# A hybrid decoder layer: key norms by selector products, packed inversion blocks, decay sums loaded a step ahead, c spread by TensorE and a closing block of 512

## The chip, the cores and the metric

One Trainium2 chip, one core. The metric is the device time of one execution in microseconds (us). Engines: PE is TensorE (matrix products; PEld are its weight loads), DVE is VectorE, ACT is ScalarE, POOL is GpSimd and SP the queue from which most DMA transfers are issued; POOL issues the others.

## The reference, cut to what matters

One decoder layer for 256 tokens of width 2048, all in fp32. Two modulations come from a condition vector c; the token mixer runs attention with 8 heads and a gated delta rule with 16 value heads beside each other; then comes a SwiGLU of inner width 5632.

```python
mod = silu(c) @ w_ada + b_ada                  # 6 x 2048: sh1, sc1, g1, sh2, sc2, g2
h = x * (1.0 + sc1) + sh1
proj = h @ w_in                                # attention q, k, v; delta q, k, v; z, b, a; two gates
y_a = moba_attention(qa, ka, va, rel_bias)     # 256 tokens: one causal block per head
qb, kb, vb = split(silu(causal_conv4(gdn_qkv)))
qb, kb = l2norm(qb) * 128 ** -0.5, l2norm(kb)
beta = sigmoid(gdn_b);  g = -exp(a_log) * softplus(gdn_a + dt_bias)
o = gated_delta_rule(qb, kb, vb, g, beta)      # decays exp(cumsum g), a triangular solve, a running state
y_b = o * rsqrt(mean(o * o) + eps) * gdn_norm_w * silu(z)
merged = sigmoid(gate_a) * (y_a @ w_proj_moba) + sigmoid(gate_b) * (y_b @ w_proj_gdn)
x = layer_norm(ALPHA * x + g1 * (merged @ w_out))
h = x * (1.0 + sc2) + sh2
x = layer_norm(ALPHA * x + g2 * ((silu(h @ w_gate) * (h @ w_up)) @ w_ffn_out))
```

## The kernel before, in words

Every large product keeps fp32 accuracy by splitting both operands into two parts of a reduced fp32 type: `split_w` lets ACT write the high part `hi` of a weight tile of 512 KB and DVE the rest `lo`, and three products (hi x hi, hi x low, lo x high) replace one. A program of steps (`step`, `do`, `run(3)`) holds one weight tile per step: SP loads it into one of six `raw` buffers, ACT and DVE split it up to three steps ahead, and PE multiplies; a step of 24 narrow products is the clock of all else. `raw_a` tiles of w_ada share the `raw` buffers; a DVE sum along them (`ada_sum`) gives one column of the modulation.

The first five groups of steps (`startup`) go through parts of w_in with as many rows of h as are ready: the sums need c, broadcast to all partitions and put through Silu (`load_c`), and `ada_opening` loads its tiles with `between` placing the first part of x and the small weights `wba` among them.

The rest of the token mixer is written as generators in lanes ("moba" for attention, "main" for gates, the delta rule's chain, its norm and transposes, "pre" for convolution, norms and the transposing of v, "ada" for sums). After each step `tick` advances them by a budget: a yielded number is a cost, `rest(n)` lets a lane pause for n steps, so that a transfer may land, and `until(flag)` waits for another lane. A planner then fixes each engine's order; engines take their instructions in that order.

For batch b of 8 value heads: `gdn_qk` sums the squares of q and k on PE (`ss`), sends the sums to DRAM (`rnd`), reads them back as 16 columns, takes the inverse roots, writes them back, and loads them broadcast to all partitions as four tiles `rb`, by which DVE multiplies `kq`. `gdn_chain` then loads, per pair of heads, the decay sums (`gr`), forms the decayed products `ma0` and `ma1`, and inverts a unit triangular matrix per head and chunk: all blocks of 128x128 go to DRAM (`mbd`), their diagonal blocks of 32x32 are gathered as `Mb`, inverted on DVE column by column, scattered to `ubd` and read back as `UU`; PE merges the blocks (`ps_mt`, `z`, `ps_a`) and applies them. Many small tiles share one tag, c2, with four buffers: `gr`, `e`, `rb`, the attention's `bias`, `z`, `tm` and others. In PSUM the tags gd and tp have two buffers each for all lanes.

The last projection (`w_fo`, 5632 rows) runs in column blocks of 512, 512, 512, 256 and 256 (`ln_blocks`); with each block DVE forms the residual, its statistics and a scaling, and after the last `finish` gives the means and inverse deviations. The closing products and eight DVE operations write the output.

## Time and profile before

| | us |
|---|---|
| median of 3 runs | 1732.25 (1728.62 to 1736.27) |
| the profiled execution | 1728.49 |
| its span in the trace | 1726.4 |
| PE, DVE, ACT busy | 1649.9, 1233.1, 831.2 |

The profiled execution has its own time, 2.1 us above the span that the trace covers. A share of busy time is an average over stages. A gap in a time line is put down to the instruction that ended it last. Matrix products overlap in the records, so a standing PE is seen in the idle time before an instruction, and a slow one in the granted clock.

### The profile page before, as it was taken

Reading aid. Unit: us, or ns where it says so; the run is one execution under the profiler, and the core shown is the slowest. Engines: PE = TensorE matmul, PEld = TensorE weight load, DVE = VectorE, ACT = ScalarE, POOL = GpSimd, SP = SyncE. Lnnn points to the kernel's source line nnn. Section 1 sums busy time; section 2 is a strip of 40 time slices with the busy share of each in tenths; the row PEclk is TensorE's granted clock in tenths of the full one; section 3 lists DMA queues with packets and bytes.
Section 4 is the critical chain, followed back from the end, with each engine's and each line's share of the span. In section 5 each row is a group of like instructions: output and inputs, shape, how many; then the busy total and the mean of one; then the engine's idle time right before and its main releaser. Section 6 shows DMA issues by size and latency. Waiting matters only on the chain.

```text
span 1726.4 us, 28691 instructions
## 1 busy us (share of the span) xinstructions
PE 1649.9 (96%) x11317; PEld 1497.8 (87%) x11317; DVE 1233.1 (71%) x1767; ACT 831.2 (48%) x1182; POOL 47.9 (3%) x78
## 2 busy tenths in 40 slices
PE   3999999989998999999999999999999999999997
PEld 3899999779987889889988998888888888888896
DVE  6899999669775568657989787666666666555454
ACT  3544455569453494346433454444444444433341
POOL 0000000111010000000000000000000000000000
PEclk9999999999998999999999999999999999999998
DMA  9999996667676667866999567777777777655651
GB/s 376 349 353 347 368 335 211 200 206 222 196 230 194 191 192 241 277 192 196 313 347 361 170 205 262 234 229 231 228 226 231 231 234 231 227 193 191 195 183 73
DMA packets 115414, 417.52 MB, mean 242 GB/s; under 512 B 13836, under 2 KB 14956, under 8 KB 109772
## 3 DMA queue, kind: packets, MB, share of 16 engines
q1 hardware_dynamic: 110464, 401.17, 68.5%
q0 software_dynamic: 4816, 14.52, 3.3%
q8 instruction: 89, 1.46, 0.3%
q14 instruction: 45, 0.37, 0.1%
HBM read 409.75 MB, written 5.89 MB: 241 GB/s over the span
## 4 chain that ended last, share of the span: by engine, by line
PE 62%; DVE 3%; DMA 3%; issue 1%; ACT 1%; DVEq 0%; POOL 0%; ACTq 0%; POOLq 0%
PE mm L307 17%; PE mm L311 8%; PE mm L348 8%; PE mm L350 7%; PE mm L349 7%; PE mm L302 4%; PE mm L301 4%; PE mm L300 4%; DMA raw_a<-in_w_ada 1%; DVE lo L216 1%; PE ps L721 1%; DMA raw<-in_w_out 1%; ACT hi L215 0%; DMA rb<-rnd 0%; DVE raw_a L235 0%
## 5 line engine op out<-in xcount | busy, mean ns | idle before, releaser
L215 ACT CAST hi<-raw 128x1024 fp32r<-128x1024 f32 (+2 forms) x576 | 582.0, 1015 | 687.6 <-PE mm L350 219.6
L216 DVE TENSOR_TENSOR lo<-raw,hi 128x1024 fp32r<-128x1024 f32 (+2 forms) x576 | 673.1, 1177 | 291.8 <-ACT hi L215 289.7
L300 PE MATMUL mm<-s,hi 128*128 128x256 f32 x1232 | 349.9, 285 | 28.4 <-ACT s L223 23.7
L302 PE MATMUL mm<-s,lo 128*128 128x256 f32 x1232 | 346.9, 282 | 4.8 <-DVE lo L216 4.7
L301 PE MATMUL mm<-s,hi 128*128 128x256 f32 x1232 | 346.8, 282 | 0.0
L307 PE MATMUL mm<-s,hi 128*128 128x512 f32 x1280 | 319.5, 392 | 0.0
L307 PEld LDWEIGHTS mm<-s,hi 128*128 128x128 f32 x1280 | 228.5, 188 | 39.4
L300 PEld LDWEIGHTS mm<-s,hi 128*128 128x128 f32 x1232 | 234.9, 191 | 30.7 <-ACT s L223 23.7
L302 PEld LDWEIGHTS mm<-s,lo 128*128 128x128 f32 x1232 | 235.0, 191 | 6.8 <-DVE lo L216 6.6
L301 PEld LDWEIGHTS mm<-s,hi 128*128 128x128 f32 x1232 | 235.9, 192 | 0.7 <-issue 0.2
L311 PEld LDWEIGHTS mm<-s,lo 128*128 128x128 f32 x1280 | 169.8, 188 | 13.6
L311 PE MATMUL mm<-s,lo 128*128 128x256 f32 x1280 | 171.9, 277 | 0.0
L348 PE MATMUL mm<-hi,ach 128*128 128x512 f32 (+1 forms) x440 | 152.6, 347 | 0.0
L350 PE MATMUL mm<-hi,acl 128*128 128x512 f32 (+1 forms) x440 | 152.5, 347 | 0.0
L349 PE MATMUL mm<-lo,ach 128*128 128x512 f32 (+1 forms) x440 | 152.5, 347 | 0.0
L235 DVE CUSTOM_DVE_ANT_0 raw_a<-raw_a,cb,cols 128x1024 f32<-128x1024 f32 x56 | 71.8, 1283 | 52.0 <-DMA raw_a<-in_w_ada 52.0
L235 DVE CUSTOM_DVE_ANT_0 raw_a<-raw_a,cb,ada_half 128x1024 f32<-128x1024 f32 x56 | 71.8, 1282 | 48.7 <-DMA raw_a<-in_w_ada 48.6
L235 DVE CUSTOM_DVE_ANT_0 r<-r,cb,cols 128x2048 f32<-128x2048 f32 x40 | 93.7, 2346 | 10.6 <-DMA r<-in_w_ada 10.6
L350 PEld LDWEIGHTS mm<-hi,acl 128*128 128x128 f32 x440 | 83.4, 189 | 10.4
L349 PEld LDWEIGHTS mm<-lo,ach 128*128 128x128 f32 x440 | 83.4, 189 | 10.4
L348 PEld LDWEIGHTS mm<-hi,ach 128*128 128x128 f32 x440 | 83.4, 189 | 10.1
L348 PE MATMUL mm<-hi,s 128*128 128x512 f32 x192 | 78.5, 409 | 0.0
(309 smaller groups left out, 2274.3 us busy)
## 6 DMA issues: line engine op xcount, KB each, us to landing
raw<-in_w_ffn_in SPq DMA_DIRECT2D x176, 512.0 KB, 4.4
raw<-in_w_in SPq DMA_DIRECT2D x160, 512.0 KB, 4.5
raw_a<-in_w_ada SPq DMA_DIRECT2D x112, 512.0 KB, 4.4
raw<-in_w_ffn_out SPq DMA_DIRECT2D x88, 512.0 KB, 4.3
r<-in_w_ada SPq DMA_DIRECT2D x40, 1024.0 KB, 8.4
raw<-in_w_in SPq DMA_DIRECT2D x48, 384.0 KB, 6.5
raw<-in_w_proj_gdn SPq DMA_DIRECT2D x32, 512.0 KB, 4.5
raw<-in_w_out SPq DMA_DIRECT2D x32, 512.0 KB, 5.6
```

Of the source, the lines that this page charges most:

```text
L215: s_.copy(hi, raw)
L216: low = v_.tensor_tensor(lo, raw, hi.bitcast(F32), op=OP.subtract)
L235: v_.tensor_tensor_reduce(out=raw, in0=raw, in1=cb[:, n * part:n * part + n], scale=1.0, scalar=cols[:, col:col + 1] if first else h, op0= ...
L300: t_.matmul(o, hi[:, i, c], ah, start=(first and i == 0 and t == 0), stop=False)
L301: t_.matmul(o, hi[:, i, c], al, start=False, stop=False)
L302: t_.matmul(o, lo[:, i, c], ah, start=False, stop=(last and i == kn - 1 and t == 1))
L307: t_.matmul(box[t].rearrange("p (u i) -> p u i", u=2), hi[:, i, t * P:(t + 1) * P], both[k0 + i], start=(first and i == 0), stop=False)
L311: t_.matmul(box[t][:, :S], lo[:, i, t * P:(t + 1) * P], both[k0 + i][:, 0, :], start=False, stop=(last and i == kn - 1))
L348: t_.matmul(box[h], xh, hi[:, i, :], start=start, stop=False)
L349: t_.matmul(box[h], xh, lo[:, i, :], start=False, stop=False)
L350: t_.matmul(box[h], xl, hi[:, i, :], start=False, stop=stop)
L721: t_.matmul(ps[to, n, :], lhs(n), rhs(n), start=True, stop=True)
```

## The change

Six edits. The condition vector is loaded as one row and spread over the partitions by four products with a row of ones; the first part of x follows the four first weight tiles and `wba` comes in the second group. The norms of q and k stay on the chip: the inverse roots are taken on all partitions, split into a high and a low part in `rows`, and selector columns (`sel`) spread them by PE into PSUM, where DVE reads them. `gr` is loaded one pair ahead. Only diagonal blocks, packed by ACT (`mc`), go through DRAM, and three rests are shorter. The squares of the output norm come before z is waited for. The closing projection has four blocks of 512, and the last block's scaling keeps its place in the program, behind `finish`.

```diff
-    c[:, C_SEL + 1] = 1.0
-    c[:, C_QS] = np.where(i < 64, SCALE, 1.0)
+    c[:, C_SEL + 1] = c[:, C_SEL + 17] = 1.0
+    c[:, C_QS] = np.where(i % 16 < 1, SCALE, 1.0)
+    c[:, C_LOW] = np.where(i % 32 < 16, 0.0, -1.0)
...
-    def load_c(i):
-        half = cb[:, 1024 * i:1024 * i + 1024]
-        dma.dma_start(half, a["c"][0, 1024 * i:1024 * i + 1024].partition_broadcast(P))
-        s_.activation(half, half, AF.Silu)
+    def load_c():
+        ones = e2("ones", [1, P])
+        v_.memset(ones, 1.0)
+        dma.dma_start(cb[0:1, :], a["c"])
+        for i in range(4):
+            ps = (pt.tile([P, 512], F32, tag="tp", name="ps_c") if i % 2 else
+                  pg.tile([P, 512], F32, tag="gd", name="ps_c"))
+            t_.matmul(ps, ones, cb[0:1, 512 * i:512 * i + 512], start=True, stop=True)
+            s_.activation(cb[:, 512 * i:512 * i + 512], ps, AF.Silu)
...
-        if n == 2:
+        if n == 2 * GROUPS[0][1]:
             load_x(*GROUPS[0])
-        elif n == 3:
-            load_ba()
...
             do(load_small)
+            do(load_ba)
...
+    def make_sel():
+        for g in range(4):
+            for u in range(2):
+                c = 32 * g + u
+                v_.tensor_tensor(sel[:, g + 4 * u:g + 4 * u + 1], ident[:, c:c + 1], ident[:, c + 16:c + 17], op=OP.add)
...
-        sr = e2("sr", [P, S])
-        s_.copy(sr, ss)
-        for g in range(4):
-            sdma.dma_start(rnd[b][g::4], sr[32 * g:32 * g + 2])
...
+        yield rest(2)
+        nr, nt = c2("nr", [P, 2, S]), c2("nt", [P, S])
+        re, rr = nr[:, 0, :], nr[:, 1, :]
+        v_.tensor_scalar(re, ss, epsc[:, 0:1], None, op0=OP.add)
+        s_.activation(rr, re, AF.Sqrt)
+        yield 0.4
+        yield rest()
+        v_.reciprocal(rr, rr)
+        v_.tensor_tensor(nt, rr, rr, op=OP.mult)
+        v_.tensor_tensor(nt, nt, re, op=OP.mult)
+        v_.tensor_scalar(nt, nt, -0.5, 1.5, op0=OP.mult, op1=OP.add)
+        v_.scalar_tensor_tensor(nt, nt, cst[:, C_QS:C_QS + 1], rr, op0=OP.mult, op1=OP.mult)
+        hi = k1.tile([P, S], F32R, tag="c2", name="nh", bufs=4)
+        s_.copy(hi, nt)
+        v_.scalar_tensor_tensor(rows, hi.bitcast(F32), cst[:, C_LOW:C_LOW + 1], nt, op0=OP.mult, op1=OP.add)
+        yield 2.2
+        for t in range(4):
+            if t % 2 == 0:
+                yield rest()
+                rbs = [pt.tile([P, 2, S], F32, tag="tp", name="rb"), pg.tile([P, 2, S], F32, tag="gd", name="rb")]
+                for x in range(2):
+                    for i in range(2):
+                        n = t + x + 4 * i
+                        t_.matmul(rbs[x][:, i, :], sel[:, n:n + 1].to_broadcast([P, P]), rows, start=True, stop=True)
+                yield 0.1
+                yield rest()
+            v_.tensor_tensor(kq[:, t::4, :], kq[:, t::4, :], rbs[t % 2], op=OP.mult)
             yield 0.6
...
-        for q in range(4):
+        def gc_rows(q):
             gr = c2("gr", [P, 2, S])
             sdma.dma_start(gr, bc_heads(gcd, 8 * b + 2 * q))
-            es = []
+            return gr
+
+        nxt = gc_rows(0)
+        yield rest(2)
+        for q in range(4):
+            gr, es = nxt, []
...
+            if q < 3:
+                nxt = gc_rows(q + 1)
...
-        md = mbd[b][:, :P, :].rearrange("(h a) j i -> j a h i", a=2)
-        sdma.dma_start(md[:, 0], ma0[:, :, 1, 0:P])
-        sdma.dma_start(md[:, 1], ma1[:, :, 1, :])
+        mc = c2("mc", [P, VH, 32])
+        for q in range(4):
+            c = slice(32 * q, 32 * q + 32)
+            s_.copy(mc[c, 0::2, :], ma0[c, :, 1, c])
+            s_.copy(mc[c, 1::2, :], ma1[c, :, 1, c])
+        sdma.dma_start(mbd[b].rearrange("n j i -> j n i"), mc)
...
-            sdma.dma_start(m[half], diag(mbd[b]))
+            sdma.dma_start(m[half], mbd[b].rearrange("n (q r) i -> (n q) r i", q=4))
...
-        yield rest(7)
+        yield rest(6)
...
-            yield rest(((12, 4), (12, 4))[b][hh])
+            yield rest(((10, 3), (10, 3))[b][hh])
...
-        yield from until(f"z{b}")
         yield from until(f"c{b}")
...
+            if h % 2 == 1:
+                yield rest()
...
+        yield from until(f"z{b}")
...
-    for n, (c0, cn) in enumerate(ln_blocks()):
+    for n, (c0, cn) in enumerate((512 * n, 512) for n in range(4)):
...
-                v_.tensor_tensor(r[:, h, cc], r[:, h, cc], cur["g"][:, cc], op=OP.mult)
+                scaled = v_.tensor_tensor(r[:, h, cc], r[:, h, cc], cur["g"][:, cc], op=OP.mult)
+                if n == 3:
+                    tc.keep_in_program_order(scaled)
```

## Rows read from the trace of the kernel before

**Rows 1.** The page's first part: busy time of each engine, its share of the span and its instructions.

```profile
PE 1649.9 (96%) x11317; PEld 1497.8 (87%) x11317; DVE 1233.1 (71%) x1767; ACT 831.2 (48%) x1182; POOL 47.9 (3%) x78
```

**Rows 2.** The waits of PE over the whole span: line, what it waited for, us in total, times, the longest.

```profile
PE mm L300 <- ACT s L223: 23.7, 1, 23.7
...
PE ps_a L745 <- DVE z L740: 8.9, 2, 8.1
PE tp L894 <- ACT pe L884: 7.7, 1, 7.7
```

**Rows 3.** The time line of PE, at four places: start and duration in us, the instruction, and in brackets the idle time of the engine before it with what ended it.

```profile
372.31 0.47 PE L894 MATMUL tp<-cst,pe 128*128 128x128 f32 x1 [7.73 <-ACT pe L884]
...
446.61 0.39 PE L302 MATMUL mm<-ya,lo 128*128 128x256 f32 x1 [2.40 <-DVE lo L216]
...
513.19 0.58 PE L302 MATMUL mm<-ya,lo 128*128 128x256 f32 x1 [3.53 <-DVE lo L216]
...
536.52 0.23 PE L745 MATMUL ps_a<-z,UU 32*32 32x32 f32 x1 [8.12 <-DVE z L740]
```

**Rows 4.** Windows behind those four gaps: the stretch and its length, busy time (and count) of PE, weight loads, DVE, ACT and POOL, then the granted clock, the DMA share and GB/s.

```profile
372.30:376.30 4.00, 3.99 (x19) 3.84 (x20) 2.37 (x4) 3.14 (x8) 0.00 (x0) 0.58 0.78 239
446.60:452.00 5.40, 5.08 (x28) 4.88 (x29) 4.92 (x18) 3.49 (x6) 0.00 (x0) 0.68 0.33 97
513.20:520.00 6.80, 6.80 (x36) 6.80 (x37) 3.46 (x9) 5.86 (x7) 0.55 (x1) 0.57 0.76 261
536.50:548.00 11.50, 11.47 (x103) 10.71 (x104) 5.03 (x8) 2.65 (x7) 0.00 (x0) 0.57 0.41 138
```

**Rows 5.** The time line of DVE ahead of 372 us, with the first and the last of four multiplications by `rb`.

```profile
358.89 0.69 DVE L625 TENSOR_TENSOR kq<-kq,rb 128x512 f32<-128x512 f32 x1 [2.52 <-DMA rb<-rnd]
...
364.23 0.69 DVE L625 TENSOR_TENSOR kq<-kq,rb 128x512 f32<-128x512 f32 x1 [0.68 <-DMA rb<-rnd]
...
365.98 0.28 DVE L871 SCALAR_TENSOR_TENSOR pe<-psS,bias 128x128 f32<-128x128 f32 x1
```

**Rows 6.** The time line of DVE ahead of 536 us, with the first of four multiplications by `rb`.

```profile
525.22 0.69 DVE L625 TENSOR_TENSOR kq<-kq,rb 128x512 f32<-128x512 f32 x1 [2.59 <-DMA rb<-rnd]
...
535.79 1.22 DVE L740 TENSOR_TENSOR z<-ps_mt,bcs 32x128 f32<-32x128 f32 x4
```

**Rows 7.** The time lines of POOL, which issues these transfers, and of DVE around 446 us.

```profile
421.14 0.91 POOL L676 DMA_DIRECT2D mbd<-ma  x1 [11.43 <-DVE ma L670]
...
436.86 1.09 POOL L683 DMA_DIRECT2D Mb<-mbd  x1 [6.10 <-issue]
...
444.19 1.22 DVE L690 SCALAR_TENSOR_TENSOR Mb<-Mb,bb 128x1024 f32<-128x1024 f32 x1 [5.92 <-DMA Mb<-mbd]
```

**Rows 8.** The time line of DVE ahead of 513 us.

```profile
510.71 1.28 DVE L235 CUSTOM_DVE_ANT_0 raw_a<-raw_a,cb,cols 128x1024 f32<-128x1024 f32 x1 [6.03 <-DMA raw_a<-in_w_ada]
```

**Rows 9.** Windows of the first stage (columns as in rows 4).

```profile
20.00:60.00 40.00, 31.21 (x216) 29.81 (x216) 32.62 (x41) 24.12 (x46) 0.00 (x0) 0.91 1.00 382
...
165.00:280.00 115.00, 114.88 (x1013) 114.68 (x1012) 110.13 (x133) 53.98 (x65) 2.57 (x4) 1.00 0.89 329
```

**Rows 10.** Groups of instructions of DVE and ACT by shape: line, operation, names, shapes, count, then busy us in all and mean ns of one, then the idle time before them.

```profile
L224 DVE TENSOR_TENSOR s<-hf,s 128x256 fp32r<-128x256 f32 x16 | 6.1, 419 | 0.3 <-ACT s L223 0.3
...
L360 DVE RECIPROCAL nr<-nr 128x16 f32<-128x16 f32 x2 | 0.5, 248 | 0.3 <-ACT nr L359 0.3
...
L520 DVE RECIPROCAL bcs<-w 128x32 f32<-128x32 f32 x1 | 0.4, 353 | 0.0
...
L605 ACT COPY sr<-ss 128x256 f32<-128x256 f32 x2 | 0.8, 376 | 0.8 <-PE ss L602 0.8
```

**Rows 11.** The DMA issues by line: queue, count, KB each, median us from issue to landing.

```profile
UU<-ubd POOLq DMA_DIRECT2D x4, 512.0 KB, 6.2
...
Mb<-mbd POOLq DMA_DIRECT2D x4, 256.0 KB, 7.1
...
ubd<-Ub POOLq DMA_DIRECT2D x4, 128.0 KB, 5.4
```

**Rows 12.** The time line of PE at one of the plain fp32 products of 512 columns, which the trace records as two instructions.

```profile
389.35 1.02 PE L665 MATMUL g<-kq 128*128 128x512 f32 x2
```

**Rows 13.** The time lines of ACT and DVE in the start: the first Silu of the condition vector, the first adaLN sum, and what follows the fourth sum.

```profile
4.84 1.06 ACT L131 ACTIVATE cb<-cb 128x1024 f32<-128x1024 f32 x1 [2.82 <-DMA cb<-in_c]
...
10.49 2.35 DVE L235 CUSTOM_DVE_ANT_0 r<-r,cb,cols 128x2048 f32<-128x2048 f32 x1 [9.59 <-DMA r<-in_w_ada]
...
21.43 0.69 DVE L216 TENSOR_TENSOR lo<-raw,hi 128x512 fp32r<-128x512 f32 x1
```

**Rows 14.** Windows of the closing projection, in its narrow and in its wide blocks (columns as in rows 4).

```profile
1647.50:1710.50 63.00, 63.00 (x528) 63.00 (x526) 31.28 (x38) 21.35 (x21) 0.00 (x0) 1.00 0.37 118
1532.00:1595.00 63.00, 63.00 (x280) 52.18 (x279) 34.64 (x35) 24.27 (x23) 0.00 (x0) 1.00 0.60 193
```

**Rows 15.** Groups of instructions of DVE by shape, of the last layer norm.

```profile
L1058 DVE BATCH_NORM_STATS2 st<-r 128x6 f32<-128x512 f32 x12 | 8.3, 688 | 0.0
...
L1058 DVE BATCH_NORM_STATS2 st<-r 128x6 f32<-128x256 f32 x8 | 3.3, 415 | 0.1
...
L1280 DVE TENSOR_TENSOR r<-r,b 128x256 f32<-128x256 f32 x4 | 1.6, 404 | 0.0
```

**Rows 16.** The time line of POOL at one of the loads of the attention bias.

```profile
402.30 0.54 POOL L866 DMA_DIRECT2D bias<-in_rel  x1 [5.10 <-ACT e L657]
```

More of the change, by code (lines that the diff above doesn't have):

```diff
@@ L452, in add_ba @@
         s_.copy(ba, ps[:32, :S])
-    load_c(0)
-    load_c(1)
+    load_c()
     dma.dma_start(cols, a["cols"])
@@ L501, in layer @@
     bcs = k1.tile([P, 5, VH], F32, name="bcs")
-    nb = k1.tile([P, 88], F32, name="nb")[:, :2 * VH].rearrange("p (u h) -> p u h", u=2)
+    nb = k1.tile([P, 2, VH], F32, name="nb")
+    rows = k1.tile([P, S], F32R, name="gnr")
+    sel = k1.tile([P, 8], F32R, name="sel")
+    def make_sel():
[3 more added lines that the diff above has]
+                v_.tensor_tensor(sel[:, g + 4 * u:g + 4 * u + 1], ident[:, c:c + 1], ident[:, c + 16:c + 17], op=OP.add)
     gcd = dr.tile([VH, S], F32, name="gcd")
@@ L571, in conv @@
             yield 2.0
-    rnd = [dr.tile([8, S], F32, name=f"rnd{b}") for b in range(2)]
-    mbd = [dr.tile([16, P + 1, P], F32, name=f"mbd{b}") for b in range(2)]
+    mbd = [dr.tile([16, P, 32], F32, name=f"mbd{b}") for b in range(2)]
     ubd = dr.tile([16, P + 1, P], F32, name="ubd")
@@ L586, in zero_dram @@
         yield 0.0
-    bvs = [None, None]
+    bvs = [v.rearrange("p f (h i) -> p h f i", h=2) for v in vts]
     def bc_heads(t, h0):
@@ L603, in gdn_qk @@
                           start=(u == 0), stop=(u == 1))
-        sr = e2("sr", [P, S])
-        s_.copy(sr, ss)
-        for g in range(4):
-            sdma.dma_start(rnd[b][g::4], sr[32 * g:32 * g + 2])
-        nr = c2("nr", [P, 3, VH])
-        rn, re, rr = [nr[:, n, :] for n in range(3)]
-        flat = bass.AP(tensor=rnd[b].tensor, offset=rnd[b].offset, ap=[[16, P], [1, 16]])
-        sdma.dma_start(rn, flat)
-        yield 0.1
-        yield rest((4, 8)[b])
-        rsqrt(rn, re, rr, rn, epsc[:, 0:1])
@@ L615, in gdn_qk @@
-        v_.tensor_scalar(rn, rn, cst[:, C_QS:C_QS + 1], None, op0=OP.mult)
-        sdma.dma_start(flat, rn)
-        yield 0.6
-        rbs = [c2("rb", [P, 2, S]) for _ in range(4)]
-        for t, rb in enumerate(rbs):
-            sdma.dma_start(rb, bass.AP(tensor=rnd[b].tensor, offset=rnd[b].offset + t * S,
-                                       ap=[[0, P], [4 * S, 2], [1, S]]))
-        yield 0.1
-        yield rest((6, 9)[b])
-        for t, rb in enumerate(rbs):
-            v_.tensor_tensor(kq[:, t::4, :], kq[:, t::4, :], rb, op=OP.mult)
+        yield 0.1
@@ L629, in gdn_v @@
         yield rest((1, 3)[b])
-        bv = vts[b].rearrange("p f (h i) -> p h f i", h=2)
-        bvs[b] = bv
+        bv = bvs[b]
         for f in range(0, 8, 2):
@@ L644, in gdn_chain @@
         yield from until(f"k{b}")
-        yield rest()
+        yield from until("gates")
         kq, bv = kqs[b], bvs[b]
@@ L806, in gdn_pre @@
             yield from zero_dram()
+            make_sel()
         yield from gdn_qk(b)
@@ L814, in gdn_norm @@
     def gdn_norm(b):
-        yield from until(f"z{b}")
         yield from until(f"c{b}")
-        o, yb = bvs[b], ybs[b]
-        ss = k1.tile([P, 2, 8], F32, tag="oss", name="oss")
+        o = bvs[b]
+        on = c2("on", [P, 4, 2, 8])
+        ss = on[:, 0]
         for h in range(8):
@@ L822, in gdn_norm @@
                 s_.activation(sq, o[:, i, h, :], AF.Square, accum_out=ss[:, i, h:h + 1])
+            if h % 2 == 1:
+                yield rest()
         v_.tensor_scalar(ss, ss, 1.0 / HD, None, op0=OP.mult)
-        rs = k1.tile([P, 2, 8], F32, tag="ors", name="ors")
-        rsqrt(rs, *[k1.tile([P, 2, 8], F32, tag="o" + n, name="o" + n) for n in "er"], ss, epsc[:, 0:1])
+        rs = on[:, 1]
+        rsqrt(rs, on[:, 2], on[:, 3], ss, epsc[:, 0:1])
         yield 0.6
+        yield from until(f"z{b}")
+        yb = ybs[b]
         for h in range(8):
@@ L1268, in fo_begin @@
         v_.memset(z.bitcast(F32), 1.0)
-        cur["st"] = perm.tile([P, 2, 5, 6], F32, tag="stt", name="st2", bufs=2)
+        cur["st"] = perm.tile([P, 2, 4, 6], F32, tag="stt", name="st2", bufs=2)
     do(fo_begin)
-    for n, (c0, cn) in enumerate(ln_blocks()):
+    for n, (c0, cn) in enumerate((512 * n, 512) for n in range(4)):
         if n == 3:
```

2 lines of the change are left out of this document (1 added, 1 removed).

## The prediction

> **What bounds the kernel now.** I read the page's busy times first: TensorE (PE) is busy 96% of the span, VectorE (DVE) 71%, ScalarE (ACT) 48% [rows 1]. So an edit pays only where it shortens PE's own work or a time in which PE stands. Second, the waits by engine, for PE: the reader is to see that few names carry them, 23.7 us before the first product and then `z` with 8.9 and a transpose with 7.7 [rows 2]. Third, the time line of PE for the place of each: the four large ones after the start lie at 372, 446, 513 and 536 us, with 7.73, 2.40, 3.53 and 8.12 us of standing [rows 3]. Fourth, the windows behind those gaps for the granted clock: 0.58, 0.68, 0.57 and 0.57 over 4.0, 5.4, 6.8 and 11.5 us, so PE ran largely at 1.2 GHz instead of 2.4 after having stood [rows 4]. At share c of the clock, a window w loses w x (1 - c): 1.7, 1.7, 2.9 and 4.9 us. With their gaps (446 has another 0.3 a little later, taken into its sum) the four places cost 9.4, 4.4, 6.4 and 13.0, together 33 us. These, the start and the end are what can be gained.
>
> Their causes, from DVE's and the DMA queues' time lines. At 372 DVE waits for `rb` four times from 356 to 364 us, and the scores `pe`, which the transpose needs, stand behind that until 365.98 [rows 5]. At 536 the same line waits 2.59 for `rb` at 525.22; PE has stood since 528.4, and the `z` that releases it comes only at 535.79 [rows 6]. At 446 DVE waits 5.92 for `Mb`, whose second half was issued only at 436.86, 15.7 us after the first write to `mbd` [rows 7]; `lo` stands behind it. At 513 DVE waits 6.03 for an adaLN weight [rows 8], which the change doesn't touch.
>
> **The change, part by part.**
>
> *Norms.* Gone: eight `rb` transfers and the round trip through DRAM ahead of them. The wait of 372 has no other cause in the rows, so its 9.4 us go. At 536 a wait of 2.59 us for `rb` and four multiplications of 0.69 stood ahead of `z`, with more such waits between them; the new code needs no transfer there and puts rests between the pairs; an adaLN sum and `lo` stay. I take 10 of 13.0 (bounds 5 and 13).
> Added on PE: 2 x 8 selector products of 256 columns. A 256-column product of the same type takes 115/1013 = 0.114 us in the full stretch [rows 9], so +1.8, and 1.9 with their weight loads.
> Added on DVE, per batch, full-width arithmetic instead of 16 columns: six operations at 0.42 each, as a 128x256 operation takes, and a reciprocal. Its rows are 0.248 for 16 and 0.353 for 32 elements, 6.5 ns for each more: 0.353 + 224 x 0.0065 = 1.8 us for 256 [rows 10]. About 4.3 against 1.4 us per batch; DVE has 29% idle and weights are split up to three steps ahead (3 x 24 x 0.114 = 8 us), which hides it. If that cover were gone, 2.9 x 2 = 5.8 us.
> The added wait: a product waits for `rows`, and behind it in PE's order stand all weight products; behind the two held PSUM tiles stand attention and transposes of the other lanes. Bounds for the four rounds (two per batch): nothing, and four times the place at 372, 37.6 us. Nearer to nothing, since the rests (a step of 2.7 us each) come ahead of each product; I take +3 for all new waits, those below included.
>
> *Packed inversion blocks.* Written: 256 KB in runs of 128 B instead of 1 MB; read: 4 KB in one run per partition, in place of runs of 128 B, whose transfers landed after 7.1 us [rows 11]. A write of 128 KB in 128 B runs landed after 5.4; for 256 KB I take 7, then 4 for the read. With 3 us for eight ACT copies (0.376 is a 128x256 copy [rows 10]; ACT has other work there) `Mb` arrives at 421 + 3 + 7 + 4 = 435. The sum asks for it one step (2.7 us) earlier than at 438.3, so about 435.6: no stall, 4 of 4.4 us go (bounds 0 and 4.4). The two shorter rests ahead of `UU` leave 10 and 3 steps, 27 and 8 us, for a transfer that landed after 6.2 [rows 11]: hidden, else one gap as at 446.
>
> The Trainium skill speaks against it: "DMA: Bandwidth & Descriptors", section Specifications, asks for at least 512 B per transfer for line rate and says that below this the engine reads, modifies and writes. By that rule the packed write loses what its fewer bytes gain; at twice the row's 5.4, 11 in place of 7 us, `Mb` comes 4 us late, the gap stays, and the sum is 4 higher. The rows show a 128 B write of 5.4 us, which covers a quarter of the old bytes, so I stay with 7.
>
> *At 513.* An uncovered transfer stays; only what ran beside it changes. 2 of 6.4 (bounds 0 and 6.4).
>
> *Decay sums a step ahead.* `gr` is now loaded before the step that needs it; no PE gap in rows 3 has it as its cause: 0. It costs a fourth buffer of the four tagged c2 (rivals).
>
> *Start.* Gone: 1 MB of broadcast and 256 KB of `wba` ahead of the weights. The broadcast's first half was there at 4.84, so 8 KB land no later; four plain fp32 products of 512 columns take 1.02 each at full clock [rows 12], 2.04 at half, then 0.6 for the last Silu: `cb` is ready between 9.5 and 13.6, I take 11. Before, the first sum started at 10.49 and the four were over at 21.43, waits for weights between [rows 13]. Now the weights land earlier and the sums run back to back: 11 + 4 x 2.38 = 20.5. PE starts 1 us earlier. From 20 to 60 us DMA is at 1.00 [rows 9], so some of the missing bytes (1 MB at 382 GB/s is 2.7 us) come off there: another 1. Together -2 (bounds +2 and -4). The eight selector columns on DVE are short and lie where PE runs full.
>
> *Closing block.* 528 products of 256 columns took 63.0 us, 0.119 each, with weight loads busy for all of it; 280 of 512 columns took 63.0, 0.225 each, with weight loads busy 52.2 [rows 14]. 264 x 0.2265 = 59.8: -3.5 with the whole block counted (63.3). Behind the last product DVE works 512 columns in place of 256 on each half: `rt`, `r` and the statistics cost like the statistics' rows, 0.69 in place of 0.42, so 6 x 0.27 = 1.6 more. Some 0.5 comes back, since the two scalings, 0.40 each by their row [rows 15] and now between these operations, are put behind `finish`, under PE's and ACT's part there. +1.1 (bounds 0 and 2); together -2.4.
>
> Another rule against: "TensorE: Matmul & The Clock Gate", section Back-to-back issue gap, gives N/2.4 + 2.5 ns for a single warm matmul, which would make two of 256 cost hardly more than one of 512 (an estimate by that page: 0.7 us saved) and the whole edit a loss of 0.4. The windows show weight loads filling the narrow stretch, so the measured 0.119 decides.
>
> *Norm of the output.* Squares before z, spread by rests: the gap there is not in rows 3; 0. The copies and squares load ACT, hidden, as it is busy 48%.
>
> **Sum:** -9.4 - 10 - 4 - 2 - 2 - 2.4 + 1.9 + 3 = -24.9. The profiled execution took 1728.5 us (span 1726.4 and 2.1 around), 3.8 below the median of 1732.25; on its footing that is 1703.6, on the median's 1707.
>
> **Rivals.**
> - *The gap moves to the c2 buffers* (0.18). `gr`, two `e` and the next `gr` fill all four; the attention bias uses the same tag and already waited 5.10 us for it [rows 16]. If one bias comes late, DVE stands in its order and PE gets one gap like that at 372: 1707 + 9.4 = 1716; against it, the `rb` tiles left the same tag.
> - *The packed write is slow* (0.07): 128 B runs cost 11 us, the gap at 446 stays, 1711. *Two narrow products cost one wide* (0.03): the closing block gains 0.7 instead of 3.5, 1710. These are the two rules above, as mechanisms here; the 5.4 and the 0.119 speak against them.
> - *It frees only waits that others fill* (0.09): at 513 and 536 the adaLN transfer is what is late next, and a new 513-like wait of 6.4 comes at each freed place: 1732 - 4.5 + 1.9 = about 1730.
> - *Slower* (0.08): the products wait for `rows` in PE's order, in all four rounds as long as the transpose at 372: 1707 + 37.6 = 1745. It decides from 25/4 = 6.2 us per round on.
>
> **How the numbers follow.** The forecast, 1707, has 0.55; its own range is 1697 to 1717. A measurement of this kernel tells 0.5% from no change, so faster means below 1723.6 and slower above 1740.9. Faster: 0.53 + 0.07 + 0.03 + 0.15 = 0.78; same: 0.14; slower 0.08. With all gaps gone at once and no new wait, -4 - 9.4 - 13 - 4.4 - 6.4 - 3.5 + 1.9 = -38.8, 1693, which leaves 1695 as the low end; the high end takes in the moved gap and part of the no-gain case: 1728.
>
> **What would show it.** No PE wait above 3 us between 330 and 560 us; no line waiting for `rb`; `Mb` waited for below 3 us; the first product at 21.5 to 23.5; the closing block's 264 products in 60 us and about 1 us more from its last product to `z`. Wrong would be PE waits on the selector products, or a transpose in the attention lane behind a bias transfer.

## The result, and the profile after

The changed kernel takes 1717.43 us (median of six executions, 1707.79 to 1720.98), the kernel before, timed beside it again, 1727.07 (six, 1723.69 to 1736.27). The ratio is 0.9933 with a 95% interval of 0.9912 to 0.9954: faster by 0.67%. Forecast were 1707 in a range of 1695 to 1728, so the side and the range hold, but the gain is 9.6 us and not 24.9. One thing has to be kept in mind with the traces: the profiled execution of the changed kernel was its fastest, 1707.79, while that of before stood near its median (1728.5). The two traces differ by 20.7 us, the medians by 9.6.

The busy times after, from the first part of the page, to be read against [rows 1]: PE has 240 instructions fewer, and the time that it is busy has hardly changed.

```profile
PE 1649.5 (97%) x11077; PEld 1480.6 (87%) x11077; DVE 1236.8 (72%) x1768; ACT 836.5 (49%) x1198; POOL 32.3 (2%) x56
```

The waits of PE over the whole span (line, what it waited for, us in total, times, longest), against [rows 2]:

```profile
PE mm L306 <- ACT s L229: 12.3, 1, 12.3
PE tp_u L758 <- DMA UU<-ubd: 5.6, 2, 4.1
...
PE tpm L1326 <- DVE z L1323: 5.1, 1, 5.1
PE g L689 <- DVE ma L694: 5.0, 2, 3.8
PE ps_c L136 <- DMA cb<-in_c: 2.6, 1, 2.6
```

None of the four gaps of [rows 3] is left: the transpose of the attention, `lo` at 446 and 513 and `z` at 536 are gone from the list. In their place stand two waits for `UU`, the longer 4.10 us, and two for `ma`, the longer 3.80 us. The time line of PE at the first product and at these places (start, duration, instruction, idle time before it and what ended it):

```profile
22.01 0.80 PE L306 MATMUL mm<-s,hi 128*128 128x256 f32 x2 [12.26 <-ACT s L229]
...
490.28 0.58 PE L758 MATMUL tp_u<-cst,UU 96*128 96x96 f32 x2 [1.47 <-DMA UU<-ubd]
...
594.52 0.70 PE L689 MATMUL g<-kq 128*128 128x512 f32 x1 [3.80 <-DVE ma L694]
...
672.40 0.42 PE L758 MATMUL tp_u<-cst,UU 96*128 96x96 f32 x1 [4.10 <-DMA UU<-ubd]
```

Behind the waits for `UU` the granted clock is between its levels, as in [rows 4]; behind the wait for `ma` it is full (windows; columns as in rows 4):

```profile
490.20:496.00 5.80, 5.72 (x49) 5.60 (x51) 2.64 (x4) 1.14 (x3) 0.00 (x0) 0.71 0.99 373
672.40:680.00 7.60, 7.60 (x71) 7.43 (x71) 1.18 (x2) 2.01 (x3) 0.00 (x0) 0.64 0.99 364
594.50:600.00 5.50, 5.48 (x22) 4.24 (x23) 4.55 (x8) 3.65 (x9) 0.00 (x0) 1.00 0.60 192
```

`Mb`, which came at 444.19 after a wait of 5.92 [rows 7], now comes at 424.25 without one. The time line of POOL and DVE:

```profile
412.35 1.20 POOL L704 DMA_DIRECT2D mbd<-mc  x1 [8.93 <-ACT mc L703]
418.46 1.05 POOL L710 DMA_DIRECT2D Mb<-mbd  x2 [4.92 <-DMA mbd<-mc]
...
424.25 1.23 DVE L717 SCALAR_TENSOR_TENSOR Mb<-Mb,bb 128x1024 f32<-128x1024 f32 x1
```

A wait that was 2.24 us in all before has grown: ACT waits for `gr`, the rows of decay sums that the change means to fetch a step ahead. From the waits of ACT:

```profile
ACT e L679 <- DMA gr<-gcd: 11.8, 4, 5.0
```

and from the waits of POOL, which issues that transfer and needs a free buffer of the tag c2 for it, here one that comes free when ACT has made `e` from an earlier `gr`:

```profile
POOL gr L668 <- ACT e L679: 51.6, 5, 22.6
```

So `gr` did not get ahead in the second batch. ACT's wait passes to `e` on DVE, from there to `ma`, and so to PE at 586 and 594 us.

### The profile page after: what moved, and what is told of

It reads as the page before. It is cut to its first block, busy times and chain, and to the rows that moved or that the text cites. A ratio compares the mean times of both kernels' runs of the same rounds, so it can differ in the third digit from the quotient of the medians.

```text
span 1706.0 us, 28192 instructions
## 1 busy us (share of the span) xinstructions
PE 1649.5 (97%) x11077; PEld 1480.6 (87%) x11077; DVE 1236.8 (72%) x1768; ACT 836.5 (49%) x1198; POOL 32.3 (2%) x56
## 3 DMA queue, kind: packets, MB, share of 16 engines
HBM read 406.59 MB, written 4.28 MB: 241 GB/s over the span
## 4 chain that ended last, share of the span: by engine, by line
PE 54%; DVE 5%; DMA 4%; issue 2%; ACT 1%; DVEq 0%; POOL 0%; ACTq 0%; POOLq 0%
PE mm L313 17%; PE mm L317 9%; PE mm L354 7%; PE mm L355 7%; PE mm L356 7%; DMA raw_a<-in_w_ada 2%; DVE lo L222 2%; PE mm L306 2%; PE mm L308 2%; PE mm L307 2%; DMA gr<-gcd 1%; DVE raw_a L241 1%; DMA raw<-in_w_out 0%; ACT hi L221 0%; PE ps L748 0%
## 5 line engine op out<-in xcount | busy, mean ns | idle before, releaser
L306 PEld LDWEIGHTS mm<-s,hi 128*128 128x128 f32 x1232 | 234.2, 190 | 23.5 <-ACT s L229 13.8
L354 PE MATMUL mm<-hi,ach 128*128 128x512 f32 x352 | 137.0, 389 | 0.0
L356 PE MATMUL mm<-hi,acl 128*128 128x512 f32 x352 | 136.9, 389 | 0.0
L355 PE MATMUL mm<-lo,ach 128*128 128x512 f32 x352 | 136.9, 389 | 0.0
L356 PEld LDWEIGHTS mm<-hi,acl 128*128 128x128 f32 x352 | 66.1, 188 | 13.8
L354 PEld LDWEIGHTS mm<-hi,ach 128*128 128x128 f32 x352 | 66.1, 188 | 13.6
L355 PEld LDWEIGHTS mm<-lo,ach 128*128 128x128 f32 x352 | 66.1, 188 | 13.6
```

Of the source, the lines that this page charges most:

```text
L306: t_.matmul(o, hi[:, i, c], ah, start=(first and i == 0 and t == 0), stop=False)
L354: t_.matmul(box[h], xh, hi[:, i, :], start=start, stop=False)
L355: t_.matmul(box[h], xh, lo[:, i, :], start=False, stop=False)
L356: t_.matmul(box[h], xl, hi[:, i, :], start=False, stop=stop)
```

## The experiments

The first group asks where the changed kernel still loses; the second takes each part of the change alone onto the kernel before; the third takes parts away or joins two. Three groups were timed, each with executions of the kernel before among its own: medians of 1727.96, 1726.85 and 1725.28. A gain below is against the median of its own group.

| kernel | median us | ratio to before, 95% interval | gain us |
|---|---|---|---|
| the change, again | 1716.83 | 0.9939 [0.9915, 0.9962] | 11.1 |
| rests of 12 and 4 | 1719.50 | 0.9942 [0.9923, 0.9962] | 8.5 |
| output norm's tiles off the c2 ring | 1709.36 | 0.9895 [0.9871, 0.9919] | 18.6 |
| both of these | 1713.35 | 0.9910 [0.9882, 0.9938] | 14.6 |
| norms alone | 1726.16 | 0.9991 [0.9969, 1.0013] | 0.7 |
| packed blocks alone | 1725.94 | 0.9999 [0.9979, 1.0018] | 0.9 |
| closing block alone | 1722.31 | 0.9971 [0.9953, 0.9989] | 4.5 |
| start alone | 1726.55 | 1.0001 [0.9985, 1.0016] | 0.3 |
| norms and packed blocks | 1712.74 | 0.9927 [0.9907, 0.9946] | 12.5 |
| off the ring, blocks not packed | 1715.25 | 0.9939 [0.9919, 0.9960] | 10.0 |
| off the ring, `gr` in its own step | 1710.85 | 0.9919 [0.9902, 0.9937] | 14.4 |
| off the ring, norms as before | 1726.36 | 1.0005 [0.9990, 1.0019] | -1.1 |

To read the traces of so many kernels side by side, I cut out the mixers, from PE's first kept product (at about 158 us) to the first transpose of the ffn, and summed from PE's time line: the standing of PE; the products of 256 columns that came some 0.21 us apart instead of 0.113 to 0.118, that is at the lower level of the clock, at 0.10 us each; and, for those at full clock, what their mean spacing adds to 0.1133 us (the last section tells of that one). What is left is, for the most part, the work itself.

| profiled execution of | mixers us | standing | at the lower clock | spacing over 0.1133 | rest |
|---|---|---|---|---|---|
| before | 816.7 | 32.8 | 10.0 | 6.8 | 767.2 |
| the change | 800.9 | 20.2 | 6.6 | 6.9 | 767.2 |
| the change, again | 816.5 | 28.7 | 7.8 | 10.4 | 769.5 |
| off the ring | 799.0 | 20.2 | 6.8 | 3.9 | 768.1 |
| norms alone | 818.2 | 29.1 | 12.5 | 10.6 | 766.0 |
| packed blocks alone | 816.7 | 34.3 | 7.6 | 5.5 | 769.3 |
| norms and packed blocks | 807.7 | 26.1 | 7.5 | 9.2 | 764.9 |
| off the ring, not packed | 809.8 | 27.7 | 12.2 | 3.7 | 766.2 |
| off the ring, norms as before | 821.6 | 36.7 | 12.8 | 4.0 | 768.0 |

The reader is to see that the rest is 765 to 770 us in all nine, whatever the kernel: what they differ by are the three columns before it, and the standing most of all. Each row is one execution, and that of the norms with the packed blocks, 1719.77 us, was the slowest of its six.

### The change once more

No edit.

> The changed kernel, unedited, for a second trace of it. Its profiled execution was 20.7 us under the profiled one of before, but its median is only 9.6 us under the median of before, and its six times run from 1707.8 to 1721.0. Theory 1: the waits that the change leaves (PE for the UU transfer, 4.1 and 1.5 us; DVE and through it PE for the gr rows, about 5 us) depend on when transfers land, and the executions that are slower lose there: a second trace that comes out at 1714 to 1720 has PE waits for UU or gr that are 5 to 12 us larger than in the first, and the ends of the stages stay within 1 us elsewhere. Rival: the loss is spread over the whole execution or lies in the stages behind the mixers (clock, transfers of weights), and the waits named stay as they were. Median expected 1717, ratio to before 0.993.

Its profiled execution took 1721.72 us. In the waits of PE the one for `UU` is twice as long (compare the list above), that for `ma` 4.4 in place of 5.0:

```profile
PE tp_u L758 <- DMA UU<-ubd: 10.6, 2, 7.7
```

Of the 15.6 us by which the mixers are longer than in the first trace, standing makes 8.5, the lower clock 1.2, the spacing 3.5 and the rest 2.3. Of the standing, 5.0 us are the waits for `UU`. So theory 1 holds for the waits for `UU` but not for those behind `gr`, which did not grow, and the rival holds for a part: some 3.5 us lie where no wait is at all.

### The rests ahead of UU, and the c2 ring

```diff
-            yield rest(((10, 3), (10, 3))[b][hh])
+            yield rest(((12, 4), (12, 4))[b][hh])
```

> The changed kernel with the rests ahead of tp_u back at 12 and 4 steps instead of 10 and 3. Theory 1 (the shorter rests bring PE to tp_u before its UU transfer has landed, 4.10 us at 672.40 and 1.47 us at 490.28, and the clock behind them stands at 0.64 and 0.71 for 7.6 and 5.8 us, some 4.4 us more): those two waits go and the time falls by 6 to 10 us against the changed kernel, to about 1709. Rival A: the two more steps only move the wait to the next thing in line (vn and the chain's own products come later, the chain is the longest thread), and the time is within 3 us of the changed kernel. Rival B: the chain is the thread that ends last and a longer rest makes it end later: 2 to 5 us slower than the changed kernel.

The median, 1719.50, is no better than that of the change (1716.83 beside it). The waits for `UU` are gone from the list, but a new one stands earlier, of DVE for `Mb` and of PE behind it (time lines of DVE and PE):

```profile
628.98 1.22 DVE L717 SCALAR_TENSOR_TENSOR Mb<-Mb,bb 128x1024 f32<-128x1024 f32 x1 [4.64 <-DMA Mb<-mbd]
```

```profile
635.59 0.58 PE L308 MATMUL mm<-s,lo 128*128 128x256 f32 x1 [9.39 <-DVE lo L222]
```

Theory 1 falls as a cause of lost time: the waits for `UU` are real, but without them the time is no shorter. Rival A, that another wait takes their place, fits this trace; between DVE's wait and `lo` lie 4.28 us of the output norm's scaling, so PE's wait is longer than DVE's. That the longer rests bring it is not shown, since with the short ones, in the kernel of the next edit, DVE waits for `Mb` nearly as long (4.40 us at 616.14). The time alone, 2.7 us over the change by the medians, would fit rival B as well.

```diff
-        on = c2("on", [P, 4, 2, 8])
+        on = b2("on", [P, 4, 2, 8])
...
-                sq = c2("osq", [P, P])
+                sq = b2("osq", [P, P])
```

> The changed kernel with the tiles of the output norm (on, osq) out of the c2 ring of four buffers, in a ring of three that is idle by then. Theory 2 (on is held in one of the four c2 buffers through the second chain, so gr cannot be asked for a step ahead: ACT waits 11.8 us in all for gr, DVE 4.16 us behind it at 591.97 and PE 5.0 us for ma): gr of the second chain is issued a step ahead, PE's 5.0 us for ma go, and the time falls by 4 to 6 us against the changed kernel, to about 1712. Rival: the ring of four is full of gr and the e tiles of the step that runs, with or without on (gr of the step ahead needs a fourth slot that the last e frees), ACT's waits for gr stay at 8 us or more, and the time stays within 2 us of the changed kernel.

The median falls by 7.5 us to 1709.36, more than expected. From the waits of ACT and of PE:

```profile
ACT e L679 <- DMA gr<-gcd: 3.0, 2, 2.1
```

```profile
PE g L689 <- DVE ma L694: 0.2, 1, 0.2
```

ACT's waits for `gr` went from 11.8 to 3.0 and PE's for `ma` from 5.0 to 0.2. Theory 2 is shown for this pair of tiles: with the output norm's small tile `on` and its squares out of the ring of four that `gr` and `e` need, the waits all but go. The change had moved `on` into that ring. The squares were there before too, but they used to wait for z, and now they begin 72 us earlier, within the second batch's chain (durations in ns, first and last start; before, then the change):

```profile
L822 ACT ACTIVATE osq<-v x32: 293/302/322, 636.0 to 790.9; 128x128 f32<-128x128 f32 x32
...
L850 ACT ACTIVATE osq<-v x32: 293/310/323, 563.9 to 752.0; 128x128 f32<-128x128 f32 x32
```

Which of the two tiles holds up `gr` was not tried apart, and PE's 4.8 us for `ma` are not all of the 7.5.

> The changed kernel with both edits: rests of 12 and 4 steps and the output norm's tiles out of the c2 ring. If both theories hold, the gains add up: 10 to 15 us under the changed kernel, about 1704. If only the rests matter, as with those alone (about 1709); if only the ring does, about 1712; if neither, 1717.

Both edits together: 1713.35, 4.0 us over the ring edit alone. The longer rests give nothing here either. The ring edit alone is the fastest kernel of this study, 0.9895 of before.

### One part alone on the kernel before

Norms alone: the code of `gdn_qk`, its constants and its tiles from the change, and the small tile `on` of the output norm in the idle ring, so that all of them fit; its squares stay in c2.

```diff
-        sdma.dma_start(rn, flat)
...
-        rbs = [c2("rb", [P, 2, S]) for _ in range(4)]
-        for t, rb in enumerate(rbs):
...
+        v_.reciprocal(rr, rr)
...
+                        t_.matmul(rbs[x][:, i, :], sel[:, n:n + 1].to_broadcast([P, P]), rows, start=True, stop=True)
```

> The kernel before with the norms alone changed: no round trip through DRAM, selector products, and the small tiles of the output norm in the idle ring of three, everything else as before (mbd unpacked, gr fetched as before, old start and closing blocks, rests of 12 and 4). By the prediction's terms: the 7.73 us at 372 and the 8.12 us at 536 with the slow clock behind each go (-9.4 and -10), the products cost +1.9, so -15 to -18 us against before, about 1711. Rival (what was freed was filled by the next wait): the gaps at 446 and 513, which this kernel keeps, grow, or the g products wait for gr; the time falls by 6 us or less, 1721 or more.

The ratio is 0.9991: the rival's. The gaps of 7.73 and 8.12 us did go, and this came instead. The time line of DVE, then that of PE:

```profile
429.68 1.22 DVE L705 SCALAR_TENSOR_TENSOR Mb<-Mb,bb 128x1024 f32<-128x1024 f32 x1 [8.02 <-issue]
...
695.26 1.28 DVE L236 CUSTOM_DVE_ANT_0 raw_a<-raw_a,cb,cols 128x1024 f32<-128x1024 f32 x1 [7.65 <-DMA raw_a<-in_w_ada]
```

```profile
384.00 0.38 PE L885 MATMUL psS<-qk 128*128 128x128 f32 x1 [2.08 <-DVE ma L685]
...
433.20 0.48 PE L918 MATMUL poa<-pT,tv 128*128 128x256 f32 x1 [2.67 <-ACT pT L913]
...
442.58 0.49 PE L302 MATMUL mm<-ya,hi 128*128 128x256 f32 x1 [2.57 <-DVE ya L225]
...
663.57 0.38 PE L303 MATMUL mm<-s,lo 128*128 128x256 f32 x1 [2.80 <-DVE lo L217]
...
697.75 0.58 PE L303 MATMUL mm<-s,lo 128*128 128x256 f32 x1 [5.08 <-DVE lo L217]
```

And of POOL, where these transfers are issued:

```profile
408.71 0.92 POOL L691 DMA_DIRECT2D mbd<-ma  x1 [2.99 <-DVE ma L685]
...
417.89 1.09 POOL L698 DMA_DIRECT2D Mb<-mbd  x1 [7.33 <-DMA mbd<-ma]
...
425.36 1.10 POOL L698 DMA_DIRECT2D Mb<-mbd  x1 [6.38 <-issue]
```

The reader is to see DVE's 8.02 us ahead of `Mb`, which was 5.92 before [rows 7]. The first write to `mbd` is issued 12.4 us earlier than at 421.14, but from there to the sum that reads `Mb` it still takes 21.0 us (23.1 before), so DVE, which comes to it sooner, stands longer. (The profile names nothing that ended this wait; in the trace the second half of `Mb`, asked for at 425.36, has landed at 429.60, just before the sum.) PE stands at 433 and 442 us behind that, and its clock shows it (windows; PE's busy time and count, then the granted clock, DMA share, GB/s):

```profile
440.00:445.00 5.00, 2.21 (x10) 0.77 0.61 206
445.00:450.00 5.00, 3.68 (x15) 0.50 0.71 215
```

The five places stand for 15.2 us; 15.85 were freed at the two of the norms, and the 3.53 at 513 went too. All standing in the mixers fell by 3.7 us, the selector products cost 2.1 of it, and this execution lost 3.8 in the spacing.

```diff
-        md = mbd[b][:, :P, :].rearrange("(h a) j i -> j a h i", a=2)
-        sdma.dma_start(md[:, 0], ma0[:, :, 1, 0:P])
-        sdma.dma_start(md[:, 1], ma1[:, :, 1, :])
+        mc = c2("mc", [P, VH, 32])
+        for q in range(4):
+            c = slice(32 * q, 32 * q + 32)
+            s_.copy(mc[c, 0::2, :], ma0[c, :, 1, c])
+            s_.copy(mc[c, 1::2, :], ma1[c, :, 1, c])
+        sdma.dma_start(mbd[b].rearrange("n j i -> j n i"), mc)
```

> The kernel before with the packed inversion blocks alone (mc copied together on ACT, one write and two reads of whole runs). By the prediction's terms: the gap at 446 (2.40 us and the clock behind it) goes, -4 us, about 1724. Rival 1 (the wait for Mb hid behind others and comes back elsewhere): within 2 us of before. Rival 2 (the write in 128 B pieces is slow): slower than before by 2 to 5 us.

The ratio is 0.9999: rival 1. The gap at 446 is gone, and the next one, which waits for the norms, has grown from 8.12 us [rows 3] to 12.14 (time line of PE):

```profile
530.78 0.23 PE L748 MATMUL ps_a<-z,UU 32*32 32x32 f32 x1 [12.14 <-DVE z L743]
```

The 4.0 us that it grew are as much as the prediction had for the gap that went.

```diff
-    for n, (c0, cn) in enumerate(ln_blocks()):
+    for n, (c0, cn) in enumerate((512 * n, 512) for n in range(4)):
...
-                v_.tensor_tensor(r[:, h, cc], r[:, h, cc], cur["g"][:, cc], op=OP.mult)
+                scaled = v_.tensor_tensor(r[:, h, cc], r[:, h, cc], cur["g"][:, cc], op=OP.mult)
+                if n == 3:
+                    tc.keep_in_program_order(scaled)
```

> The kernel before with the closing blocks alone changed (four of 512 columns in place of five). The two traces of before and after differ by 2.7 us between the start of the ffn's transposes and the last products, so -2 to -3 us, about 1725. The rival (the closing is hidden by what the earlier parts leave, so the gain shows only with the rest of the change): within 1 us of before.

The ratio is 0.9971 [0.9953, 0.9989], which is 1.9 to 8.1 us. The trace is sharper. The two groups of PE that begin and end the ffn, with the first and last start of each, before and with this edit:

```profile
L1141 PE MATMUL tpn<-cst,r x32: 270/273/328, 976.4 to 1011.8; 128*128 128x128 f32 x32
...
L1292 PE MATMUL tpm<-cst,z x2: 378/400/421, 1715.0 to 1715.2; 128*5 128x128 f32 x2
```

```profile
L1141 PE MATMUL tpn<-cst,r x32: 270/273/331, 971.8 to 1007.2; 128*128 128x128 f32 x32
...
L1294 PE MATMUL tpm<-cst,z x2: 378/398/418, 1707.1 to 1707.3; 128*5 128x128 f32 x2
```

From the first start of the one to the first of the other are 738.6 and 735.3 us. Over all traces this distance is 738.1 to 738.8 in the five kernels with the old blocks and 735.3 to 736.0 in the nine with the new: 2.7 us, which nothing behind it takes back.

```diff
-        half = cb[:, 1024 * i:1024 * i + 1024]
-        dma.dma_start(half, a["c"][0, 1024 * i:1024 * i + 1024].partition_broadcast(P))
-        s_.activation(half, half, AF.Silu)
+        dma.dma_start(cb[0:1, :], a["c"])
+        for i in range(4):
...
+            t_.matmul(ps, ones, cb[0:1, 512 * i:512 * i + 512], start=True, stop=True)
+            s_.activation(cb[:, 512 * i:512 * i + 512], ps, AF.Silu)
```

> The kernel before with the start alone changed: c fetched once and spread by TensorE, the b and a weights made behind another group. By the traces of before and after the stage that starts at 159 to 161 us is 1.9 us earlier: -2 us, about 1726. Rival (the mixers behind it wait for things that the start doesn't bring earlier, so it is lost at the next wait): 0 to -0.5 us.

The ratio is 1.0001: the rival's. In its trace the mixers start 1.5 us earlier than before, and the second of the gaps that wait for the norms is 1.7 longer (time line of PE, against [rows 3]):

```profile
534.25 0.23 PE L748 MATMUL ps_a<-z,UU 32*32 32x32 f32 x1 [9.81 <-DVE z L743]
```

### Two parts together, and parts taken away

The kernel before with the norms and the packed blocks, the two diffs above:

> The kernel before with the norms and the packed inversion blocks both changed, nothing else. Alone, the norms left the median at 0.9991 and the packed blocks at 0.9999 of before. Theory (the two edits cover each other: with the norms alone DVE waits 8.02 us for Mb at 429.68 and PE loses 2.67 and 2.57 us behind it at 433 and 443, with the clock at half; with the packed blocks alone the norm waits of 7.02 and 12.14 us stay): together they give what neither gives alone, -5 to -9 us against before, 1718 to 1722. Rival (the gain of the whole change lies in other parts, the decay sums a step ahead and the squares of the output norm ahead of z): as with the norms alone, 1724 to 1727.

1712.74 us, 12.5 below before, more than was expected of the theory: two edits that alone give 0.7 and 0.9 us give 12.5 together. DVE's wait for `Mb` has shrunk from 8.02 to 0.84, and the clock behind it stays full (time line of DVE, windows of PE):

```profile
426.37 1.23 DVE L708 SCALAR_TENSOR_TENSOR Mb<-Mb,bb 128x1024 f32<-128x1024 f32 x1 [0.84 <-DMA Mb<-mbd]
```

```profile
440.00:445.00 5.00, 2.94 (x22) 1.00 0.76 229
445.00:450.00 5.00, 5.00 (x45) 1.00 0.37 127
```

The rival, that the gain lies in other parts of the change, falls.

The kernel off the ring, its blocks not packed (the diff of the packed blocks above, undone, and the rest ahead of the sum at 7 steps again instead of 6):

> The whole change with the output norm's tiles in the idle ring, but without the packed inversion blocks (two writes of all of ma's columns and reads of strided blocks, as before). Reference: the same with packed blocks, 1709.4. Theory (the edits cover each other): the wait for Mb comes back, 3 to 8 us on DVE, and the time rises by 4 to 8 us, 1713 to 1717. Rival (the packed blocks give nothing here either): within 2 us, 1707 to 1711.

1715.25, 5.9 above the same with packed blocks (7.6 by the ratios, as the two were timed in different groups), as the theory said. The waits of DVE for `Mb` are back, in both batches:

```profile
DVE Mb L714 <- DMA Mb<-mbd: 7.1, 1, 7.1
DVE Mb L714 <- issue: 6.0, 1, 6.0
```

The kernel off the ring, with `gr` asked for in its own step:

```diff
-        def gc_rows(q):
+        for q in range(4):
             gr = c2("gr", [P, 2, S])
             sdma.dma_start(gr, bc_heads(gcd, 8 * b + 2 * q))
...
-        nxt = gc_rows(0)
-        yield rest(2)
-        for q in range(4):
-            gr, es = nxt, []
+            es = []
...
-            if q < 3:
-                nxt = gc_rows(q + 1)
```

> The whole change with the output norm's tiles in the idle ring, but with each gr asked for in its own step as before. Reference 1709.4. Theory (asking a step ahead is what took ACT's waits for gr from 11.8 to 3.0 us and PE's for ma from 5.0 to 0): the waits for gr come back and the time rises by 3 to 6 us, 1712 to 1715. Rival (it was the freed buffers alone, and the order of asking matters little): within 2 us, 1707 to 1711.

1710.85 against 1709.36: 1.5 us by the medians, 4.1 by the ratios, with intervals that overlap. ACT's waits for `gr` are 6.5 us here and 3.0 there, and the waits of the products `g` for `ma` are 0.2 in both. But here a product of the attention stands behind `ma`, which has no such wait there (waits of PE):

```profile
PE psS L894 <- DVE ma L688: 2.1, 1, 2.1
```

So the freed buffers are what ended the wait at `g`, as the rival has it; whether asking early is worth another 1 to 4 us stays open.

The kernel off the ring, with the norms through DRAM as before (the diff of the norms, undone):

> The whole change with the output norm's tiles in the idle ring, but with the norms through DRAM as before (rb by DMA, no selector products). Reference 1709.4. Theory (the norms are what the rest needs): the waits for rb come back at about 365 and 525 with 5 to 12 us each on PE and the clock at half behind them, and of the gain of 17.5 us only the closing's 4 to 5 and a little more is left: 1718 to 1723. Rival (the norms matter as little as they did alone): 1709 to 1713.

1726.36 us: nothing of the gain is left. The ffn is as short as in the change, but the mixers are 4.9 us longer than in the trace of before. That is beyond the theory's 1718 to 1723, on its side, and only in part by the waits that it named. DVE's for `rb` are small (5.6 us in all); of the two places of PE the first is back, a little under the 5 us named, the second is not (time line of PE):

```profile
362.35 0.47 PE L910 MATMUL tp<-cst,pe 128*128 128x128 f32 x1 [4.49 <-ACT pe L900]
```

For the rest DVE stands for `Mb`, though it is packed; from the waits of DVE:

```profile
DVE Mb L702 <- DMA Mb<-mbd: 12.6, 2, 10.5
```

The shorter rests and the order of the change stay in this kernel, and which of them costs what without the early norms was not tried.

## Why the prediction was right or wrong

The side and the range held, but not the sum: the gain is 9.6 us where it had 24.9. The time, 1717.43, lies just above the forecast's own range (1697 to 1717) and nearest to the rival of the moved gap (1716). What kept it inside the whole range is that its high end, 1728, took in that rival and part of the no-gain case. Some of it is luck: the forecast stood on the median of three executions, 1732.25; from the 1727.07 of the six the same sum gives 1702. Its first sign, no wait of PE above 3 us between 330 and 560 us, came true; the two above 3 lie behind, at 594 and 672 us.

*The start* (-2): the first product came at 22.01, 1.66 us earlier than at 23.67, inside the 21.5 to 23.5 given, and the first sum at 10.42. The step was right, its worth was not: alone it gives 0.3 us by the medians, and in its trace the wait for `z` grew by what it had won.

*Norms* (-9.4 and -10). The working was right in its parts: the reciprocal of 256 elements took 1.754 us (1.8 reckoned), the six others 0.29 to 0.48 (0.42), the selector products 2.1 to 3.2 us in the time lines (1.9), and the rows of before that wait for `rb` are gone. By form, on DVE and PE of the changed kernel:

```profile
L624 DVE RECIPROCAL nr<-nr 128x256 f32<-128x256 f32 x2 | 3.5, 1754 | 0.5 <-ACT nr L621 0.5
```

```profile
L640 PE MATMUL rb<-gnr,sel 128*128 128x256 f32 x16 | 4.1, 361 | 1.8 <-DVE pe L904 1.1 <-DVE gnr L631 0.7
```

The rival "slower" fell with it: PE waited 1.8 us in all at these products, where 6.2 per round would have decided. Wrong was to book the two gaps as gains of this part: norms alone gained 0.7.

*Packed blocks* (-4). `Mb` came without a wait. The packed write landed after 5.0 us in place of 7 and the read after 5.0 in place of 4 (medians); from the issue of the write to the sum it took 11.9 us where 11 were reckoned. That the sum came before the 435.6 of the prediction is because the write was issued at 412.35 and not at 424. The Trainium skill's rule for small pieces ("DMA: Bandwidth & Descriptors", section Specifications) did not decide here: pieces of 128 B landed after 5.0 us, not after the 11 that I had worked out as that rival. The DMA issues of the changed kernel, against [rows 11]:

```profile
Mb<-mbd POOLq DMA_DIRECT2D x4, 256.0 KB, 5.0
...
mbd<-mc POOLq DMA_DIRECT2D x2, 256.0 KB, 5.0
```

What the packing takes away is one transfer in a row of three. In all five traces without it, the second half of `Mb` is asked for only when the first has landed (at 436.86 after 429.65 before, at 425.36 after 417.89 with the norms alone); in all nine with it, both halves are asked for 0.5 us apart (the row x2 at 418.46). So in the first batch the way from the first write to the sum fell from 23.1 us to 11.9. The landing of one read is not what differs: its medians are 3.5 to 7.5 us in the traces with packed blocks, 5.2 to 7.1 in those without. Why the second half had to wait is not shown.

Alone the part gained 0.9, together with the norms some 12 in place of nothing. So the sum failed where it added the terms of norms and packed blocks as if each gap stood by itself. For norms, packed blocks, selector products and new waits it had -9.4 - 10 - 4 + 1.9 + 3 = -18.5; measured together are -12.5, alone -0.7 and -0.9. The rival "it frees only waits that others fill" (0.09) describes each part alone.

*Decay sums a step ahead* (0). This is the step that failed in the change as it is. I booked no cost, since no gap of before had `gr` as its cause, and wrote that it needs a fourth buffer of c2. That was the place, and I did not count who else sits there: the change moves the small tile of the output norm onto the same tag and brings its squares, which were there, forward into the second batch's chain. The term of the output norm, also 0, looked at ACT's load and not at the ring. `gr` came late, PE stood 5.0 us, and off the ring the kernel is 7.5 us faster. The rival "the gap moves to the c2 buffers" (0.18, 1716) had the ring and nearly the time, but named the attention's bias as what comes late. No transpose of the attention stood behind a bias; `ma` did.

*At 513* (-2): the gap is not in the trace of after. I had seen no reason for more than 2. The norms alone already remove it, the packed blocks alone do not (3.12 us at 508.86); what in the norms does it no run shows.

*Shorter rests* ahead of `UU` were called hidden. They are not (5.6 and 10.6 us of waits). The rests of 27 and 8 us were set against the transfer alone, and the trace has `UU` asked for only at 483.13 and 667.38, 7.15 and 5.02 us before PE's products, when the writes of `Ub` that it reads had landed. But longer rests gain nothing, so the term of 0 was right for a wrong reason.

*Closing block* (-2.4): measured 2.7. The windows of the last block and of the ones before it show nearly one cadence, 257 and 282 products in 58.5 and 63.5 us (columns as in rows 4), and the wait from the last product to `tpm` rose from 4.29 to 5.09 us, by 0.8 where 1.1 was booked. The 0.2265 us a product of the sum stands in none of its rows, which give 0.225; with that the block would be 0.4 us shorter:

```profile
1568.00:1631.50 63.50, 63.50 (x282) 52.60 (x281) 34.80 (x35) 25.19 (x25) 0.00 (x0) 1.00 0.62 195
1631.50:1690.00 58.50, 58.11 (x257) 47.80 (x255) 27.38 (x27) 19.85 (x20) 0.00 (x0) 1.00 0.39 122
```

So a narrow product costs more than half of a wide one here, 0.119 against 0.225 us [rows 14]. By the Trainium skill's formula for an isolated product ("TensorE: Matmul & The Clock Gate", section Back-to-back issue gap) two narrow ones would cost hardly more than one wide one, which these blocks do not show. The same section of the Trainium skill says that in a stream of weight loads and products both set the spacing and that the formula counts too little for narrow ones; with that the narrow blocks agree. That it counts too much for wide ones, as the section also says, the wide blocks do not bear out (0.225 us measured, 0.216 by the formula, an estimate by that page).

*What stays open.* Off the ring the gain is 18.6 of 24.9. Norms with packed blocks, closing block and start, measured apart, make 12.5 + 4.5 + 0.3 = 17.3 of it; the early squares of the output norm were never run alone. What is missing to 24.9 I put down to waits that took the place of others, which the standing of 20.2 us in its mixers allows; that is argued and not shown, and which of them could still go was not tried.

## What to carry to other kernels

A gap is a gain only if what comes next is early as well: before gaps of several lanes are added up, move each releaser forward and ask which transfer, with an end that does not move, is met next. Two edits can be worth nothing alone and 12 us together, so a part that measures as nothing may still have to stay. When a change fetches something ahead into a ring of buffers, list every tile that takes a slot of that ring and how long each holds it.

## What the runs showed of the hardware

At full granted clock and without a single wait, PE ran the same 256-column products at either of two paces. The same stretch of the same kernel, 180 to 300 us, in its first trace and in its second (windows of PE: busy time and count, clock, DMA share, GB/s):

```profile
180.00:300.00 120.00, 120.00 (x1061) 1.00 0.83 296
```

```profile
180.00:300.00 120.00, 120.00 (x1022) 1.00 0.81 290
```

In the time lines the starts lie 0.1133 us apart in the one and 0.1178 in the other, all through. Over the 1247 products that run from about 166 to 310 us without a break this makes 5.3 us, and four of the 14 traces had the longer spacing there. Later in the same execution it may be the other: in the first trace of the change some 400 products from 621 to 668 us are 0.1178 apart. The table of the mixers has between 3.7 and 10.6 us from it. What sets it I don't know. It may be a part of why executions of one kernel differ by 10 us and more; that was not tested, but it is a reason to compare medians of many executions and not two traces.
